# A two-layer hybrid trunk: state-space input tables built on VectorE from turned factors, the last low parts queued first, and cosine products into rotated tiles

## The chip, the cores and the metric

The kernel runs on one core of a Trainium2 chip, in one launch. The metric is the time of that launch in device microseconds (us). Engines are named as the profile names them: PE is TensorE (PEld its weight loads), DVE is VectorE, ACT is ScalarE, POOL is GpSimd, SP is SyncE, whose queue issues nearly all DMAs here. Each engine works through its own instructions in the order in which the program lists them; a scheduler in the language fixes that order when the kernel is built, from priorities and dependencies.

## The reference

Input x is (1, 1024, 1024) in float32: 1024 frames of width 1024. Each layer adds a mixer of the RMS-normalised input; a last RMS norm ends it.

```python
# layer 0: one projection feeds both branches
y_a = s5_mixer(u)            # diagonal complex state space, 64 groups of 16 inputs and 64 states,
                             #   chunks of 64 frames, then gelu and a GLU with glu_w
y_b = retention(q, k, v)     # 8 heads, q and k rotated: [x1*cos - x2*sin, x1*sin + x2*cos]
x = x + concat(y_a * silu(g_a), y_b * silu(g_b)) @ w_out
# layer 1: conformer convolution module
u = a * sigmoid(b)           # h @ w_c gives a, b and a gate
x = x + (swish(norm(causal_depthwise_conv31(u))) * silu(g)) @ w_out_c
out = rmsnorm(x)
```

The state space in closed form is: the states of a chunk are sums over its frames of powers of a complex number times an input vector (bb_re, bb_im) times u, so the kernel needs tables that are products of a power factor P and an input factor B.

## The kernel before, in words

Activations stand transposed: channels on the 128 partitions, frames along the free axis, in two halves of 512. Every projection goes block by block of 128 output channels. To reach float32 accuracy each weight block is loaded in float32 (tile wf), rounded on ACT to a high part wh, and the rest, wf − wh, is the low part wl, made by DVE or POOL; the activations are split likewise. A product is three matmuls (mm3: high by high, high by low, low by high), so a half block is 24 matmuls of 128x512 and a block 48. The list made in plan() fixes the order of the weight blocks, and wnext() starts each load two blocks ahead. wf, wh and wl have three buffers each. LO_V lists the names whose low part DVE makes; all others are POOL's. Blocks in TWICE are needed for both halves of the frames at different times: their low part is stored to DRAM the first time and loaded again (wload_again) the second. For the blocks woc3_1 and woc4_1 of the last projection this reload goes into two tiles of another pool, in two pieces each.

Layer 0 runs in stages. First come eight blocks of u, then sixteen gate blocks (g), with the state space between them: one batch of eight groups for every two gate blocks. For a batch, s5_tables makes on POOL (outer, six products and sums of 128x512 a pair) the tables Mr and Mi, Tc and Ts, W3, and s5_states uses them: TensorE turns Mr and Mi (eight transposes of 128x128 against the identity, L707), ACT copies the result to W2 (L709), and W2 times U (the batch's input, loaded from DRAM at L700) gives v. DVE rotates v by Tc and Ts, scans it along the free axis and rotates back, which gives the states S. TensorE also multiplies Mr and Mi by c (kp, L752), DVE completes it (Kg), TensorE turns it (kt, L758); it goes to DRAM and comes back as the direct table W1. s5_out of the batch before then makes y on TensorE.

Then retention: for each of four pairs of heads k and q are projected (raw), a copy with its 32-row groups swapped (swp) is made by four DMAs through SP's queue, POOL multiplies raw by the cosine and swp by the sine table, and DVE adds the two into krot or qrot, which TensorE reads in sp, ktp and ro. The core of turn() in ret_proj is

```python
for b in range(4):
    s = b ^ 1
    nc.sync.dma_start(swp[32 * b:32 * b + 32, :], raw[32 * s:32 * s + 32, :])
cs = [slice(h * HALF, (h + 1) * HALF) for h in range(2)]
for c in cs:
    nc.gpsimd.tensor_tensor(raw[:, c], raw[:, c], tab[:, 0, c], op=ALU.mult)
    nc.gpsimd.tensor_tensor(swp[:, c], swp[:, c], tab[:, 1, c], op=ALU.mult)
return o, [lambda c=c: nc.vector.tensor_tensor(o[:, c], raw[:, c], swp[:, c], op=ALU.add) for c in cs]
```

After the GLU comes the output projection (wos and wor blocks, mm_wo), then layer 1: a, b and gate blocks, the convolution with 31 taps on DVE, POOL and ACT, its norm, and the last projection mm_oc (w_out_c), whose result is added to the stored x (x1l, loaded at L1316). The last three blocks of the second half are worked in quarters of 256 frames. For each quarter final_norm sums the squares on TensorE (rf_ps), takes the root, spreads it over the partitions (a diagonal tile rf_dg and a matmul, rf_R), and multiplies the eight blocks (fo), which two by two go to the output.

Of the kernel before, what the change touches and what calls it, by code (L numbers as in the profile page):

```python
# [11 lines left out]
F32 = mybir.dt.float32  # L12
# [7 lines left out]
P = 128  # L20
D = 1024
T = 1024
KB = 8
# [6 lines left out]
WARM = 14  # L30
WAIT = 8
TWICE = ("wo", "cb", "ca", "cg")
LO_V = {f"g{i}" for i in range(1, 10)} | {"u4", "u5", "u6"}
G0 = 3
# [16 lines left out]
class Trunk:  # L51
# [22 lines left out]
    def plan(self):  # L74

        A = self.A
        seq = [(A["w_ab"][nb], f"u{nb}") for nb in range(8)]
        seq += [(A["w_ab"][nb], f"g{nb}") for nb in range(8, 24)]
        for p in range(4):
            seq += [(A["w_ab"][28 + p], f"k{p}"), (A["w_ab"][24 + p], f"q{p}")]  # L80

            if p == 0:
                seq += [(A["w_v"][j], f"v{p}_{h}_{j}") for h in range(2) for j in range(4)]
            elif p > 1:
                seq += [(A["w_v"][2 * p + i], f"v{p}_{i}") for i in range(2)]
# [15 lines left out]
        self.low_load = {}  # L101
        self.wnames, self.lo_d = {n for _, n in seq}, {}
# [10 lines left out]
    def wload(self, src, name):  # L113
# [5 lines left out]
        tiles = None  # L119
        for tiles in self.wload_pieces(src, name, 1, [self.nc.vector if name[:2] in LO_V else self.nc.gpsimd]):  # L120
            done = tiles or done
# [5 lines left out]
    def wload_again(self, src, name, low):  # L127
# [6 lines left out]
        if name in ("woc3_1", "woc4_1"):  # L134

            tiles = [self.op_tile(self.opA, "A1", f"wl{i}_{name}") for i in range(2)]
            for i, t in enumerate(tiles):
                nc.sync.dma_start(t[:].bitcast(F32), low[:, i * HALF:(i + 1) * HALF])
            return wh, Halves(tiles)
        wl = self.wp.tile([P, KB, P], F32R, name=f"wl_{name}", tag="wl", bufs=3)  # L140
        self.low_load[name[:-2]] = nc.sync.dma_start(wl[:].rearrange(fl).bitcast(F32), low)
        return wh, wl
# [83 lines left out]
    def layer0_front(self, st):  # L226
# [138 lines left out]
        for nb in range(5, 8):  # L365
            u_block(nb)
        self.s5_tab, self.s5_back, self.s5_last = {}, {}, None
        self.s5_tables(0)
        for nb in range(8, 24):
# [71 lines left out]

    def rstd(self, parts, pool, name):
# [9 lines left out]
        self.spread(rp[:, :n], r4, pool, name)  # L452
        return rp
# [201 lines left out]
    def outer(self, B, o_r, o_i, ar, ai, br, bi, view, op_r=ALU.subtract, op_i=ALU.add):  # L655

        gp = self.nc.gpsimd
        for o, op, (a0, b0), (a1, b1) in ((o_r, op_r, (ar, br), (ai, bi)), (o_i, op_i, (ar, bi), (ai, br))):
# [3 lines left out]
            yield gp.tensor_tensor(o, o, t[:], op=op)  # L662

    def s5_tables(self, B):

# [20 lines left out]
        self.s5_last = self.chained(chain(*made), self.s5_last)  # L686
        R8 = self.big(f"R8_{B}", "R8", 2)
        for q in range(4):
            nc.scalar.mul(R8[:, q, :], self.m01[:], self.r8[:, 4 * B + q:4 * B + q + 1])
        self.s5_tab[B] = Mr, Mi, W3, Tc, Ts, R8  # L690

    def s5_states(self, B):
        nc, w = self.nc, self.s5
        gp, v = nc.gpsimd, nc.vector
        q0 = 4 * B
        Mr, Mi, W3, Tc, Ts, R8 = self.s5_tab.pop(B)


        U = w.tile([P, 8, P], F32, name=f"U_{B}", tag="U", bufs=2)
        nc.sync.dma_start(U[:], self.u_d[B].rearrange("j h g m -> (j h) g m"))  # L700


        W2 = []
        for nm, M in (("r", Mr), ("i", Mi)):
            ps = self.bank(f"w2{nm}_{B}")
# [59 lines left out]
        nc.sync.dma_start(Wd[:], bass.AP(tensor=kd.tensor, offset=kd.offset, ap=[[P, P], [16 * P, 8], [1, P]]))  # L765
        W1 = w.tile([P, 8, P], F32, name=f"W1_{B}", tag="W1", bufs=2)
        nc.scalar.copy(W1[:].rearrange("p g (i h) -> p i g h", i=8), Wd[:].rearrange("p i (g h) -> p i g h", g=8))
# [74 lines left out]
    def ret_proj(self, pair):  # L842
# [15 lines left out]
        def turn(nm, behind=None):  # L858
# [3 lines left out]
            for b in range(4):  # L862
                s = b ^ 1
                nc.sync.dma_start(swp[32 * b:32 * b + 32, :], raw[32 * s:32 * s + 32, :])
            cs = [slice(h * HALF, (h + 1) * HALF) for h in range(2)]
            for c in cs:
                nc.gpsimd.tensor_tensor(raw[:, c], raw[:, c], tab[:, 0, c], op=ALU.mult)
                nc.gpsimd.tensor_tensor(swp[:, c], swp[:, c], tab[:, 1, c], op=ALU.mult)
            return o, [lambda c=c: nc.vector.tensor_tensor(o[:, c], raw[:, c], swp[:, c], op=ALU.add) for c in cs]

# [170 lines left out]
    def layer0_back_and_layer1(self, st):  # L1041
# [269 lines left out]
        def w_out_c(h, nb, cols, hold=None):  # L1311
# [10 lines left out]
            def part(c):  # L1322
                ps = self.bank(f"mm_oc{nb}_{h}_{c.start}", aux=False)
                n = c.stop - c.start
                self.gemm(ps[:, :n], w, [(a[:, c], b[:, c]) for a, b in zs[h]], hold)
                v.tensor_tensor(t[:, c], ps[:, :n], xt[:, c], op=ALU.add)
                nc.scalar.activation(sq[:, c], t[:, c], AF.Square)
# [7 lines left out]
        def final_norm(h, c):  # L1335
            n = c.stop - c.start
            end = h and c.stop == HALF
            R = lp.tile([P, HALF], F32, name=f"RF_{h}_{c.start}", tag="dg", bufs=1)
            rp = self.rstd([final[h][nb][1][:, c] for nb in ((0, KB - 1) if h else (0,))], lp, f"rf_{h}_{c.start}")
            for nb in range(8):  # L1340
                if nb == 1 and not end:
                    nc.scalar.copy(R[:, :n], rp[:, :n])
# [30 lines left out]
        for h in range(2):  # L1373
# [26 lines left out]
            with self.at(410000):  # L1400
                blocks(1, range(3))
                with self.tc.issue_after(self.last_mm.ins):
                    final_norm(0, *full)
                blocks(1, range(3, 5))
            with self.at(430000):
# [11 lines left out]
                next(last[2])  # L1417
                final_norm(1, quarters[1])

# [97 lines left out]
```

## Time and profile before

| what | value |
|---|---|
| runs | 1215.86, 1223.36, 1215.69 us (median 1215.86) |
| profiled execution | 1215.57 us, span in the profile 1213.8 us |
| mean granted clock of TensorE | 0.995 of full speed |
| busy | PE 99%, PEld 83%, DVE 62%, ACT 40%, POOL 55% |
| DMA | 227.11 MB, mean 187 GB/s |

The span runs from the first to the last instruction or transfer that the profiler saw; the execution's own time lies 1.8 us above it. A view of the waits lists what each engine stood idle for; the chain follows the work that ended last back from the end, so that a step on it is a step that delays the end; a row of the timeline gives start, duration, engine, source line, operation, what is written from what, tile sizes, and in brackets the idle time before it with what ended it. In the views of windows each engine's busy time is followed by its count of instructions, then come the granted clock, the share of DMA time and GB/s.

### The profile page before, as it was taken

The numbers are of one execution on the slowest core, as the hardware profiler recorded it, in microseconds if no ns is written. First come the engines' busy times: TensorE is split into PE (matmuls) and PEld (weight loads), VectorE is DVE, ScalarE is ACT, GpSimd is POOL, SyncE is SP. The second block draws the span as 40 slices with busy tenths as digits, with TensorE's granted clock in tenths as the row PEclk, the third lists the DMA queues.
The fourth block names the chain that finished last, engine by engine and source line by source line (L and its number), as shares of the span: only waits on it lengthen the run. The fifth ranks groups of instructions, "written<-read, shape, count | busy, mean of one in ns | idle before, by whom it ended". The sixth has DMA issues, their size and how long they took to land.

```text
span 1213.8 us, 17240 instructions
## 1 busy us (share of the span) xinstructions
PE 1196.5 (99%) x6468; PEld 1001.8 (83%) x6468; DVE 751.7 (62%) x1337; ACT 479.9 (40%) x706; POOL 663.4 (55%) x457
## 2 busy tenths in 40 slices
PE   9999999999999999999999999999999999999997
PEld 7888888888888888998888788888888888888876
DVE  7966655555412457467647101699999799999523
ACT  7212233332223222234334322545535675434652
POOL 2059988888237153243443551678453567758642
PEclk9999999999999999999999999999999999999998
DMA  8342433333385165567447877766678654366763
GB/s 334 104 139 72 148 131 127 125 128 137 107 286 174 53 208 150 164 206 256 158 140 225 284 267 255 243 208 203 216 241 278 209 190 156 113 190 228 254 246 131
DMA packets 100515, 227.11 MB, mean 187 GB/s; under 512 B 9296, under 2 KB 38224, under 8 KB 99792
## 3 DMA queue, kind: packets, MB, share of 16 engines
q1 hardware_dynamic: 100432, 226.01, 56.0%
q8 instruction: 51, 0.84, 0.3%
q14 instruction: 32, 0.26, 0.1%
HBM read 160.51 MB, written 61.28 MB: 183 GB/s over the span
## 4 chain that ended last, share of the span: by engine, by line
PE 92%; DMA 3%; DVE 2%; ACT 1%; POOL 1%; issue 1%; SPq 0%; DVEq 0%; ACTq 0%; POOLq 0%
PE mm_g L165 7%; PE mm_g L166 7%; PE mm_g L164 7%; PE mm_wo L166 5%; PE mm_wo L164 5%; PE mm_wo L165 5%; PE mm_b L165 2%; PE mm_b L166 2%; PE mm_a L165 2%; PE mm_a L166 2%; PE mm_b L164 2%; PE mm_a L164 2%; PE mm_u L166 2%; PE mm_u L165 2%; PE mm_u L164 2%; PE mm_glu L164 2%
## 5 line engine op out<-in xcount | busy, mean ns | idle before, releaser
L1214 DVE SCALAR_TENSOR_TENSOR cv<-u,convw,cv 128x512 f32<-128x512 f32 x398 | 273.3, 749 | 11.9 <-ACT cv L1200 9.6
L1194 POOL TENSOR_TENSOR tp<-tp,tp 128x512 f32<-128x512 f32 x64 | 83.0, 1297 | 44.1 <-ACT tp L1193 43.0
L166 PE MATMUL mm_g<-xh,wl_g 128*128 128x512 f32 x256 | 100.8, 394 | 0.0
L165 PE MATMUL mm_g<-xl,wh_g 128*128 128x512 f32 x256 | 100.6, 393 | 0.0
L164 PE MATMUL mm_g<-xh,wh_g 128*128 128x512 f32 x256 | 100.5, 393 | 0.0
L1193 ACT ACTIVATE tp<-u,convw 128x512 f32<-128x512 f32 x64 | 45.7, 720 | 35.4 <-POOL tp L1194 33.8
L347 DVE TENSOR_TENSOR gt<-mm_g,R 128x512 f32<-128x512 f32 x32 | 21.9, 684 | 59.9 <-PE mm_g L166 59.9
L165 PEld LDWEIGHTS mm_g<-xl,wh_g 128*128 128x128 f32 x256 | 48.1, 188 | 11.3 <-issue 1.6
L166 PE MATMUL mm_oc<-zh,wl_woc 128*128 128x512 f32 (+1 forms) x152 | 54.7, 363 | 2.7 <-DMA wl_woc<-lo_woc 2.7
L156 POOL TENSOR_TENSOR wl_v<-wf_v,wh_v 128x1024 fp32r<-128x1024 f32 x12 | 29.0, 2424 | 51.3 <-ACT wh_v L155 51.3
L166 PEld LDWEIGHTS mm_g<-xh,wl_g 128*128 128x128 f32 x256 | 48.0, 188 | 10.6
L164 PEld LDWEIGHTS mm_g<-xh,wh_g 128*128 128x128 f32 x256 | 48.1, 188 | 9.6
L164 PE MATMUL mm_oc<-zh,wh_woc 128*128 128x512 f32 (+1 forms) x152 | 55.0, 367 | 0.0
L165 PE MATMUL mm_oc<-zl,wh_woc 128*128 128x512 f32 (+1 forms) x152 | 54.4, 360 | 0.3 <-POOL zl L1039 0.3
L1114 DVE TENSOR_TENSOR x<-mm_wo,xr 128x512 f32<-128x512 f32 x16 | 11.1, 691 | 70.3 <-PE mm_wo L166 49.8
L1086 POOL TENSOR_TENSOR yg<-yg,yn 128x512 f32<-128x512 f32 x16 | 21.7, 1357 | 55.8 <-PE mm_glu L166 16.0
L166 PE MATMUL mm_wo<-yrh,wl_wor 128*128 128x512 f32 x128 | 50.0, 391 | 0.8 <-POOL wl_wor L156 0.8
L165 PE MATMUL mm_u<-xl,wh_u 128*128 128x512 f32 x128 | 50.1, 391 | 0.6 <-DVE xl L279 0.6
L164 PE MATMUL mm_g<-h1h,wh_cg 128*128 128x512 f32 x128 | 50.4, 394 | 0.0
L164 PE MATMUL mm_wo<-yrh,wh_wor 128*128 128x512 f32 x128 | 50.3, 393 | 0.0
L164 PE MATMUL mm_glu<-yh,wh_glu 128*128 128x512 f32 x128 | 50.3, 393 | 0.0
L164 PE MATMUL mm_b<-h1h,wh_cb 128*128 128x512 f32 x128 | 50.2, 392 | 0.0
(400 smaller groups left out, 3626.6 us busy)
## 6 DMA issues: line engine op xcount, KB each, us to landing
wf_g<-w_ab SPq DMA_DIRECT2D x16, 512.0 KB, 4.1
wf_wos<-w_out SPq DMA_DIRECT2D x16, 512.0 KB, 5.3
wf_wor<-w_out SPq DMA_DIRECT2D x16, 512.0 KB, 5.7
wf_cb<-w_c SPq DMA_DIRECT2D x16, 512.0 KB, 4.7
wf_ca<-w_c SPq DMA_DIRECT2D x16, 512.0 KB, 4.7
wf_woc<-w_out_c SPq DMA_DIRECT2D x16, 512.0 KB, 5.3
wf_v<-w_v SPq DMA_DIRECT2D x12, 512.0 KB, 4.7
wf_cg<-w_c SPq DMA_DIRECT2D x11, 512.0 KB, 4.5
```

What stands on the lines that cost most here:

```text
L156: lo[i].tensor_tensor(wl[:].rearrange(fl)[:, c], wf[:, c], h.bitcast(F32), op=ALU.subtract)
L164: nc.tensor.matmul(ps, wh[:, kb, :], xh, start=start, stop=False)
L165: nc.tensor.matmul(ps, wh[:, kb, :], xl, start=False, stop=False)
L166: self.last_mm = nc.tensor.matmul(ps, wl[:, kb, :], xh, start=False, stop=stop)
L347: nc.vector.tensor_tensor(gt[:, c], ps[:], self.R[:, c], op=ALU.mult)
L1086: gp.tensor_tensor(yg[:], yg[:], yn[:], op=ALU.mult)
L1114: v.tensor_tensor(t[:], ps[:], xt[:], op=ALU.add)
L1193: nc.scalar.mul(sk[:], u[:, k:k + HALF], cw[:, nb, k:k + 1])
L1194: gp.tensor_tensor(s0[:], s0[:], sk[:], op=ALU.add)
L1214: v.scalar_tensor_tensor(dst[:], *tap, accs_[i][:], op0=ALU.mult, op1=ALU.add)
```

## The change

It consists of five edits.

1. From the third batch on (B > 1) W2 is no longer turned on TensorE from Mr and Mi. s5_turned() turns the small factors once, by twelve transposes, and stores them to DRAM; s5_w2() loads them spread over the partitions (four DMAs of 256 KB a batch, listed behind the load of U) and DVE makes W2 with four products, a difference and a sum, each of 128x512. To make room, R8 and W1 have one buffer in place of two.
2. In turn() the cosine product goes into the rotated tile, ahead of the sine products; DVE adds in place.
3. The low parts of wos and wor are made by DVE.
4. The reloaded low parts of woc3_1 and woc4_1 are listed ahead of the other reloads of that kind and ahead of the x1l loads of the last three blocks.
5. The first quarter's final norm stops after four blocks and goes on behind the last sum of x; in the second quarter five matmuls of ones stand between the sums and the spreading.

```diff
+IDLE = 5
-LO_V = {f"g{i}" for i in range(1, 10)} | {"u4", "u5", "u6"}
+LO_V = {f"g{i}" for i in range(1, 10)} | {"u4", "u5", "u6", "wos", "wor"}
...
-                nc.sync.dma_start(t[:].bitcast(F32), low[:, i * HALF:(i + 1) * HALF])
+                self.early_low = nc.sync.dma_start(t[:].bitcast(F32), low[:, i * HALF:(i + 1) * HALF])
...
-        self.low_load[name[:-2]] = nc.sync.dma_start(wl[:].rearrange(fl).bitcast(F32), low)
+        with self.tc.issue_after(self.early_low.ins) if self.early_low else nullcontext():
+            self.low_load[name[:-2]] = nc.sync.dma_start(wl[:].rearrange(fl).bitcast(F32), low)
...
+        if idle:
+            wait = self.bank(f"{name}_wait", aux=False)
+            with self.tc.issue_after(self.last_stat.ins):
+                for _ in range(idle):
+                    self.last_idle = nc.tensor.matmul(wait[:, :P], self.ones[:], self.ones[:], start=True, stop=True)
...
+    def s5_turned(self):
+        self.pt_d = self.dram.tile([2, 2, P, P], F32, name="pt_d")
+        self.bt_d = self.dram.tile([2, 4, P, P], F32, name="bt_d")
+        order = [self.big(f"hq{c}", "tmpV", 4) for c in range(2)]
+        for o, t in zip(order, (self.bbr, self.bbi)):
+            nc.scalar.copy(o[:].rearrange("p a (h q) -> p (a h) q", h=4), t[:].rearrange("p q h -> p h q"))
+        for i, (dst, parts) in enumerate((...)):
+            ps = self.bank(f"turn{i}")
+            for a, src in enumerate(parts):
+                nc.tensor.transpose(ps[:, a * P:(a + 1) * P], src, self.ident[:])
+            t = self.big(f"turned{i}", "tmpV", 4)
+            nc.scalar.copy(t[:].rearrange("p q n -> p (q n)"), ps[:])
+            nc.sync.dma_start(dst, t[:])
+
+    def s5_w2(self, B):
+        (ptr, pti), (btr, bti) = ([self.big(f"{n}{c}_{B}", f"{n}{c}", 1) for c in "ri"] for n in ("PT", "BT"))
+        with self.tc.issue_after(self.u_load.ins):
+            for c, (pt, bt) in enumerate(((ptr, btr), (pti, bti))):
+                nc.sync.dma_start(pt[:].rearrange("p q n -> p (q n)"),
+                                  bass.AP(tensor=dp.tensor, offset=dp.offset + (c * 2 * P + 4 * B) * P,
+                                          ap=[[32 * P, 8], [0, 16], [1, 4 * P]]))
+                nc.sync.dma_start(bt[:].rearrange("p q n -> p (q n)"),
+                                  bass.AP(tensor=db.tensor, offset=db.offset + (c * 4 * P + 4 * B) * P,
+                                          ap=[[0, 8], [32 * P, 16], [1, 4 * P]]))
+        w2r, w2i = (self.big(f"W2{nm}_{B}", f"W2{nm}", 1) for nm in "ri")
+        v.tensor_tensor(w2r[:], ptr[:], btr[:], op=ALU.mult)
+        v.tensor_tensor(w2i[:], ptr[:], bti[:], op=ALU.mult)
+        v.tensor_tensor(ptr[:], pti[:], bti[:], op=ALU.mult)
+        v.tensor_tensor(pti[:], pti[:], btr[:], op=ALU.mult)
+        v.tensor_tensor(w2r[:], w2r[:], ptr[:], op=ALU.subtract)
+        v.tensor_tensor(w2i[:], w2i[:], pti[:], op=ALU.add)
+        return [w2r, w2i]
...
-        self.s5_tab[B] = Mr, Mi, W3, Tc, Ts, R8
+        self.s5_tab[B] = Mr, Mi, W3, Tc, Ts, R8, self.s5_w2(B) if B > 1 else None
...
-        W2 = []
-        for nm, M in (("r", Mr), ("i", Mi)):
+        first, W2 = W2 is None, W2 or []
+        for nm, M in (("r", Mr), ("i", Mi)) if first else ():
...
             for c in cs:
-                nc.gpsimd.tensor_tensor(raw[:, c], raw[:, c], tab[:, 0, c], op=ALU.mult)
+                nc.gpsimd.tensor_tensor(o[:, c], raw[:, c], tab[:, 0, c], op=ALU.mult)
+            for c in cs:
                 nc.gpsimd.tensor_tensor(swp[:, c], swp[:, c], tab[:, 1, c], op=ALU.mult)
-            return o, [lambda c=c: nc.vector.tensor_tensor(o[:, c], raw[:, c], swp[:, c], op=ALU.add) for c in cs]
+            return o, [lambda c=c: nc.vector.tensor_tensor(o[:, c], o[:, c], swp[:, c], op=ALU.add) for c in cs]
...
-            nc.sync.dma_start(xt[:], self.x1_d[rows(nb), hs(h)])
+            with self.tc.issue_after(self.early_low.ins) if h and nb > 4 else nullcontext():
+                nc.sync.dma_start(xt[:], self.x1_d[rows(nb), hs(h)])
...
             for nb in range(8):
+                if nb == 4:
+                    yield
...
                 with self.at(420000):
-                    final_norm(1, quarters[0])
+                    first = final_norm(1, quarters[0])
+                    next(first)
...
-                final_norm(1, quarters[1])
+                with self.at(425000), self.tc.issue_after(self.last_add.ins):
+                    for _ in first:
+                        pass
+                for _ in final_norm(1, quarters[1]):
+                    pass
```

More of the change, by code (lines that the diff above doesn't have):

```diff
@@ L119, in wload @@
         tiles = None
-        for tiles in self.wload_pieces(src, name, 1, [self.nc.vector if name[:2] in LO_V else self.nc.gpsimd]):
+        for tiles in self.wload_pieces(src, name, 1, [self.nc.vector if name[:2] in LO_V or name[:3] in LO_V else self.nc.gpsimd]):
             done = tiles or done
@@ L367, in layer0_front @@
         self.s5_tab, self.s5_back, self.s5_last = {}, {}, None
+        self.s5_turned()
         self.s5_tables(0)
@@ L451, in rstd @@
         rp = self.bank(f"{name}_R")
-        self.spread(rp[:, :n], r4, pool, name)
+        with self.tc.issue_after(self.last_idle.ins) if idle else nullcontext():
+            self.spread(rp[:, :n], r4, pool, name)
         return rp
@@ L1338, in final_norm @@
             R = lp.tile([P, HALF], F32, name=f"RF_{h}_{c.start}", tag="dg", bufs=1)
-            rp = self.rstd([final[h][nb][1][:, c] for nb in ((0, KB - 1) if h else (0,))], lp, f"rf_{h}_{c.start}")
+            rp = self.rstd([final[h][nb][1][:, c] for nb in ((0, KB - 1) if h else (0,))], lp, f"rf_{h}_{c.start}",
+                           IDLE if end else 0)
             for nb in range(8):
+                if nb == 4:
+                    yield
                 if nb == 1 and not end:
```

25 lines of the change are left out of this document (17 added, 8 removed).

## The prediction

> **What bounds the kernel now.** I read the page first (busy shares, chain), then TensorE's waits, then the chain that ended last in order of time, then the timelines around its few steps that are not TensorE.
>
> ```profile
> span 1213.8 us, 17240 instructions
> PE 1196.5 (99%) x6468; PEld 1001.8 (83%) x6468; DVE 751.7 (62%) x1337; ACT 479.9 (40%) x706; POOL 663.4 (55%) x457
> ...
> PE 92%; DMA 3%; DVE 2%; ACT 1%; POOL 1%; issue 1%; SPq 0%; DVEq 0%; ACTq 0%; POOLq 0%
> ```
>
> TensorE (PE) is busy 99% of the span and holds 92% of the chain. VectorE (DVE) and GpSimd (POOL) have room on average. So work that moves onto DVE costs nothing by itself, and only two things shorten the kernel: matmuls that disappear and TensorE's stalls. The stalls that this change can touch are few:
>
> ```profile
> PE mm_oc L166 <- DMA wl_woc<-lo_woc: 2.7, 2, 2.3
> PE sp L972 <- DVE qrot L869: 1.8, 1, 1.8
> PE ro L999 <- DVE sc L978: 0.9, 1, 0.9
> PE mm_wo L166 <- POOL wl_wor L156: 0.8, 1, 0.8
> PE rf_ps L421 <- DVE fo L1352: 0.6, 1, 0.6
> ```
>
> The columns are the total in us, the number of times and the longest. Together they are 6.8 us, which already caps what the change can do beside the matmuls it takes out.
>
> **Part 1: state-space tables on DVE.** A batch now turns its two input tables with eight 128x128 transposes. The rows give their price and the batch period, 303.94 − 274.43 = 29.5 us:
>
> ```profile
> 274.43 0.44 PE w2r L707 x4
> 274.87 0.44 PE w2i L707 x4
> ...
> 303.94 0.44 PE w2r L707 x4
> ```
>
> Six batches lose 0.88 us each, −5.3 us; the new s5_turned adds 12 transposes of 0.11 us, +1.3. TensorE saves **−4.0** us (−4.6 at most, if the change of shape costs 0.1 us a batch more, which no row shows alone). ScalarE loses 12 copies and gains five; it is far from the path.
>
> The price is on DVE: six 128x512 products or sums a batch, between the steps of the scan. Both their inputs lie in SBUF, and there the trace shows DVE and POOL excluding each other. In the order DVE, POOL, DVE, POOL, DVE, POOL:
>
> ```profile
> 224.53 0.69 DVE L728 TENSOR_TENSOR v<-v,Tc 128x512 f32<-128x512 f32 x1
> 226.37 1.10 POOL L660 TENSOR_TENSOR o<-s_bbi,s_pr 128x512 f32<-128x512 f32 x1
> ...
> 233.50 1.56 DVE L156 TENSOR_TENSOR wl_g<-wf_g,wh_g 128x1024 fp32r<-128x1024 f32 x1
> 233.95 2.41 POOL L660 TENSOR_TENSOR o<-s_e2i,s_e1r 128x512 f32<-128x512 f32 x1
> ...
> 441.23 2.86 DVE L869 TENSOR_TENSOR krot<-kraw,kswp 128x512 f32<-128x512 f32 x1 [1.18 <-POOL kswp L868]
> 441.16 2.38 POOL L156 TENSOR_TENSOR wl_v<-wf_v,wh_v 128x1024 fp32r<-128x1024 f32 x1
> ```
>
> The step v, with one input in PSUM, takes 0.69 us. The step krot began just after a POOL subtraction and ended 0.55 us after it: it waited, then ran. In the second pair POOL waited for DVE. So a W2 step costs 0.6 us plus what is left of the POOL operation (1.1 to 1.4 us in this stage): 0.6 to 2.0 us, and I take 1.2, with a whole wait for the one that follows another directly. DVE's sum per batch is then:
>
> ```profile
> 215.50:245.00 29.50, 29.50 (x204) 24.67 (x202) 15.66 (x23) 9.08 (x18) 23.72 (x19) 1.00 0.36 128
> ```
>
> The third and fifth busy times are DVE and POOL. DVE goes from 15.7 to about 24 us of the new period of 28.6, POOL, delayed 0.6 us by each step, from 23.7 to 27.3. Both fit. For TensorE three deadlines count after the v matmuls of a batch:
>
> ```profile
> 233.33 0.38 SPq L700 DMA_DIRECT2D U<-u_d  x1
> 1125.28 0.45 PE mm_oc L164 x2
> ```
>
> (1) kt stands after 33 gate matmuls in the changed order, 0.6 + 33 x 0.225 = 8.1 us after v; its input Kg waits behind two W2 steps on DVE and is ready at about 6.2, at 7.6 with 2.0 us a step. (2) The load of U for the next batch, now 10.1 us after v, stands on SP's queue behind the store of a gate block whose second half DVE evacuates behind all six steps: issued at about 20, landed at about 24.5 (a load took 4.6 us in part 4's rows), needed by v at 26.7. With 2.0 us a step it comes at about 27.5, up to 1 us late. (3) The four broadcast loads of 256 KB follow U and wait for the tables' last readers; they land near 26.5 and are needed at 28.7, when the first W2 step reaches the head of DVE. The weight load behind them comes some 6 us later than now, needed two blocks later. So I add nothing for stalls; the other bound is 1 us in each of six batches, +6.
>
> [...]
>
> **Part 2: the rotation.** The chain at the one stall of the attention stage:
>
> ```profile
> 444.69 5.31 DMA qswp<-qraw
> 450.31 1.13 issue
> 451.45 1.28 POOL qswp L868
> 452.73 1.25 POOL qraw L867
> 453.98 1.69 POOL qswp L868
> 455.69 2.83 DVE qrot L869
> 458.65 0.46 PE sp L972 x2
> ```
>
> After the swap lands, POOL now runs four products, since the cosine product overwrote raw in place and had to wait for the swap that reads it. Writing it into the rotated tile lets two of the four run while the swap is under way, so two of 1.25 us leave the chain: −2.5 us against a stall of 1.8: **−1.8**, margin 0.7. The new wait is that POOL's product must wait for TensorE's readers of the previous rotated pair, with weight subtractions of 2.4 us queued behind. In the changed order these products stand behind the previous pair's sine products, so I expect no stall; bounds 0 and −2.7 (with the 0.9 of ro, which hangs on another DVE queue).
>
> **Part 3: sixteen low parts to DVE.**
>
> ```profile
> L156 POOL TENSOR_TENSOR wl_wor<-wf_wor,wh_wor 128x1024 fp32r<-128x1024 f32 x8 | 19.6, 2445 | 14.5 <-PE mm_wo L166 7.2 <-ACT wh_wor L155 5.4 <-DMA lo_wor<-wl_wor 1.8
> 630.00:760.00 130.00, 128.96 (x569) 105.63 (x568) 36.39 (x47) 43.37 (x60) 53.80 (x31) 1.00 0.73 248
> ```
>
> A part takes 2.4 us on POOL; the same shape took 1.56 on DVE beside POOL (the wl_g row of part 1). DVE is busy 36 of the 130 us there and takes some 25 more. Most of the 0.8 us wait goes: **−0.7** (0 to −0.8).
>
> **Part 4: last low parts queued first.** On SP's queue the last four (L138) stood behind a load that waits for a buffer:
>
> ```profile
> 1153.38 0.33 SPq L132 DMA_DIRECT2D wf_woc<-w_out_c  x1
> 1167.26 0.32 SPq L141 DMA_DIRECT2D wl_woc<-lo_woc  x1
> 1167.63 1.85 SPq L138 DMA_DIRECT2D wl_woc<-lo_woc  x4
> ...
> 1167.63 4.62 DMA wl_woc<-lo_woc
> 1172.30 0.79 PE mm_oc L166
> 1173.09 0.43 PE mm_oc L164
> ...
> 1170.00:1175.00 5.00, 2.70 (x6) 2.15 (x7) 0.87 (x2) 3.80 (x6) 1.26 (x1) 0.67 0.92 304
> ```
>
> They are now issued right after 1153.4 and land by about 1161, before TensorE's 1170. The 2.7 us stall goes. It also goes with a clock drop: in this window the granted clock is 0.67 and a matmul takes 0.43 us where it takes 0.225 at 1125.28; from 1172.3 to 1175 that is some 1.3 us lost. The x1l loads that are moved behind are needed only from about 1177. Sum **−3.8** (−2.3 if a smaller late load remains, −4.1 at most).
>
> **Part 5: the tail.** The last sum of x now stands ahead of three of the fo products of the first quarter:
>
> ```profile
> 1202.07 1.75 DVE L1352 TENSOR_TENSOR fo<-x,rf_R 128x256 f32<-128x256 f32 x5 [0.44 <-ACT RF L1342]
> ...
> 1203.73 0.42 DVE L1326 TENSOR_TENSOR x<-mm_oc,x1l 128x256 f32<-128x256 f32 x1
> ...
> 1203.96 1.35 PE L421 MATMUL rf_ps<-ones,s2q 128*128 128x64 f32 x8 [0.65 <-DVE fo L1352]
> ...
> 1206.48 1.19 PE L440 MATMUL rf_R<-rf_dg,ones 128*128 128x256 f32 x2 [1.17 <-DVE rf_dg L438]
> ```
>
> The sum moves 0.4 us forward, but rf_ps waits for the last fo, which reads the bank it takes: three fo of 0.35 us after the sum end near 1204.85, so rf_ps starts about 1.0 later and, its eight parts then together, ends 0.8 later. Five dummy matmuls fill the 1.28 us before rf_R. If they keep the clock, rf_R takes 0.6 instead of 1.19 us; if the clock drops under them they delay it. Bounds −0.6 and +1.8; I take **+0.9**.
>
> **Sum.** −4.0 − 1.8 − 0.7 − 3.8 + 0.9 = −9.4 us. The profiled execution took 1215.57 us, 1.8 outside its span, and is 0.3 below the median 1215.86 of the runs. That gives 1206.2 on its scale and 1206.5 on the median's, 0.8% faster. A measurement of this kernel can tell about 1% from no change (below 1203.7, above 1228.0).
>
> **Rivals.** (a) *More than that.* Every part is at its better bound: −4.6 − 2.7 − 0.8 − 4.1 − 0.6 = −12.8, 1203.1 on the median's scale, just past the mark of 1%. For it: no row forbids any of them. Against: it needs all at once, and the waits quoted above leave nothing further to gain. Chance 0.12.
> (b) *Part of the gain turns into new waits.* The U loads are within 2.2 us of their deadline; with the +6 of part 1 the time is 1212.5, with half of it and half of the two stalls of parts 2 and 4 back 1212, so 1209 to 1214. For it: the krot row. Against: POOL idles 5.8 of 29.5 us per batch, so not every step meets it. Chance 0.22.
> (c) *Slower: DVE becomes the bound of the state-space stage.* With d us a step, DVE needs 15.7 + 6d of 28.6 us, so it decides from d = 2.15; at 2.4 the six batches lose 9 us and the gain is gone. At the 2.86 of krot, if every step meets an operation as long, they lose 25 us: 1231.8 with the other gains kept. For it: krot and qrot do wait so. Against: POOL's operations in this stage are 1.1 to 1.4 us, not 2.4. Chance 0.11.
> (d) *The early queue does nothing*: the low parts wait for their own tiles or for bandwidth; then part 4 brings nothing and the time is 1210.3. For it: 1.0 MB lands in one stretch at 304 GB/s in the quoted window. Against: at 1153 nothing but one weight load stands before them. Chance 0.05, inside the range.
>
> **How the numbers follow.** The forecast, 1203.7 to 1209, has 0.50. The range 1203 to 1219 holds it with (b), (d) and nearly all of (a) and the beginning of (c), leaving out some 0.12. The chances of faster by over 1%, within 1% and slower by over 1% are 0.10 (most of a), 0.81 and 0.09 (most of c).
>
> **What would show it.** Right: no w2r rows from the third batch on; no sp<-qrot, mm_oc<-DMA and mm_wo<-wl_wor rows in TensorE's waits; a granted clock of 1.00 around 1160 to 1170; W2 steps of about 1.2 us and a period of 28.6. Wrong: TensorE waiting at v for U, at kt for Kg or at v for W2; W2 steps over 2 us; a new DMA wait behind the moved x1l; the tail from the last gate of mm_oc to the end longer by over 2 us.

## The result, and the profile after

Six runs of the changed kernel took 1203.16 to 1205.3 us, median 1204.53; those of the kernel before beside them have a median of 1216.09. The ratio is 0.9892, 95% interval [0.9871, 0.9914]: 1.1% faster, 13.1 us by the ratio and 11.6 by the medians. A second set in a later comparison gave 0.9898 [0.9879, 0.9918]. The forecast time of 1206.5 us is 2.0 too long and the direction is right. My main case is wrong: the change can be told from none, since neither interval comes near 1.00, and both ratios lie just past the 1% that I said it would stay within. How far past is not settled: both intervals reach over the 1% mark, and by the medians alone the change is 0.95%.

The page after, busy shares and chain:

```profile
span 1203.5 us, 17285 instructions
PE 1191.8 (99%) x6442; PEld 999.4 (83%) x6442; DVE 799.5 (66%) x1389; ACT 477.5 (40%) x699; POOL 637.9 (53%) x441
...
PE 95%; DMA 2%; DVE 1%; ACT 1%; issue 0%; POOL 0%; SPq 0%; DVEq 0%; POOLq 0%; ACTq 0%
```

The profiled execution took 1205.3 us, 10.3 less than the one profiled before. TensorE's share of the chain that ended last went from 92 to 95%, and DVE is busier by 48 us without costing anything. TensorE's waits, all of them:

```profile
PE rf_ps L424 <- DVE fo L1412: 1.6, 1, 1.6
PE idle L257 <- DVE mhalf L203: 1.1, 1, 1.1
PE mm_oc L168 <- DMA wl_woc<-lo_woc: 1.0, 2, 0.7
PE mm_u L167 <- DVE xl L281: 1.0, 1, 1.0
PE mm_oc L167 <- POOL zl L1095: 0.5, 1, 0.5
PE ro L1055 <- DVE sc L1034: 0.5, 1, 0.5
```

The rows of sp, wl_wor and the 2.3 us of lo_woc are gone; rf_ps grew from 0.6 to 1.6, as foreseen. In the state-space stage, one new period of 28.65 us (columns as before: the third and fifth busy times are DVE and POOL), and DVE's steps in it:

```profile
215.50:244.15 28.65, 28.65 (x195) 23.85 (x197) 22.79 (x28) 8.12 (x16) 25.40 (x19) 1.00 0.58 177
...
217.52 0.68 DVE L710 TENSOR_TENSOR W2r<-PTr,BTr 128x512 f32<-128x512 f32 x1
220.62 1.59 DVE L711 TENSOR_TENSOR W2i<-PTr,BTi 128x512 f32<-128x512 f32 x1
222.13 1.07 DVE L810 TENSOR_TENSOR Kg<-Kg,s_s_dd 128x16 f32<-128x16 f32 x1
224.32 0.76 DVE L712 TENSOR_TENSOR PTr<-PTi,BTi 128x512 f32<-128x512 f32 x1
227.25 1.05 DVE L713 TENSOR_TENSOR PTi<-PTi,BTr 128x512 f32<-128x512 f32 x1
228.23 1.77 DVE L714 TENSOR_TENSOR W2r<-W2r,PTr 128x512 f32<-128x512 f32 x1
232.90 1.62 DVE L715 TENSOR_TENSOR W2i<-W2i,PTi 128x512 f32<-128x512 f32 x1
```

The six steps take 0.7 to 1.8 us, 1.25 on average (forecast 1.2): those that meet a POOL operation wait for its end (W2i at 220.62 ends 0.55 us after a POOL operation that ended at 221.66), and the difference right behind a product waits longest, 1.75 to 1.91 us in all six batches. DVE needs 22.8 us of the period, POOL 25.4 (forecast 24 and 27.3). The tail after:

```profile
1193.46 1.07 DVE L1412 TENSOR_TENSOR fo<-x,rf_R 128x256 f32<-128x256 f32 x3
...
1194.68 1.08 PE L424 MATMUL rf_ps<-ones,s2q 128*128 128x64 f32 x8 [1.60 <-DVE fo L1412]
1195.59 1.33 PE L457 MATMUL rf_wait<-ones 128*128 128x128 f32 x10
...
1196.93 0.67 PE L443 MATMUL rf_R<-rf_dg,ones 128*128 128x256 f32 x2
```

### The profile page after: what moved, and what is told of

Its sections match the earlier page's. It is cut to its first block, busy times and chain, and to the rows that moved or that the text cites. A ratio compares the mean times of both kernels' runs of the same rounds, so it can differ in the third digit from the quotient of the medians.

```text
span 1203.5 us, 17285 instructions
## 1 busy us (share of the span) xinstructions
PE 1191.8 (99%) x6442; PEld 999.4 (83%) x6442; DVE 799.5 (66%) x1389; ACT 477.5 (40%) x699; POOL 637.9 (53%) x441
## 4 chain that ended last, share of the span: by engine, by line
PE 95%; DMA 2%; DVE 1%; ACT 1%; issue 0%; POOL 0%; SPq 0%; DVEq 0%; POOLq 0%; ACTq 0%
PE mm_g L166 7%; PE mm_g L167 7%; PE mm_g L168 7%; PE mm_wo L168 5%; PE mm_wo L166 5%; PE mm_wo L167 5%; PE mm_b L167 2%; PE mm_b L168 2%; PE mm_a L167 2%; PE mm_a L168 2%; PE mm_b L166 2%; PE mm_a L166 2%; PE mm_u L168 2%; PE mm_u L167 2%; PE mm_u L166 2%; PE mm_glu L166 2%
## 5 line engine op out<-in xcount | busy, mean ns | idle before, releaser
L1270 DVE SCALAR_TENSOR_TENSOR cv<-u,convw,cv 128x512 f32<-128x512 f32 x398 | 273.4, 751 | 11.9 <-ACT cv L1256 9.6
L393 POOL TENSOR_TENSOR s1q<-s1q,s1q 128x512 f32<-128x512 f32 x12 | 17.5, 1455 | 78.2 <-ACT s1q L388 78.2
L168 PE MATMUL mm_a<-h1h,wl_ca 128*128 128x512 f32 x128 | 50.2, 392 | 0.0
```

The costliest lines, as they stand in the source:

```text
L168: self.last_mm = nc.tensor.matmul(ps, wl[:, kb, :], xh, start=False, stop=stop)
L393: nc.gpsimd.tensor_tensor(a, a, sq[:], op=ALU.add)
L1270: v.scalar_tensor_tensor(dst[:], *tap, accs_[i][:], op0=ALU.mult, op1=ALU.add)
```

## A table of stages

A time to 0.2% does not say which part brought what. So I compare, for each profiled execution, the start of the same matmuls. Each column is a stretch between two of them (ss is the first sum of squares; the other names are those of the text above), each number how much longer (+) or shorter (−) that stretch is than in the first profile of the kernel before, in us.

| execution | start to ss | state space, to y of the last batch | to mm_q behind sp | to mm_glu behind ro | output projection, to r_ps | to mm_oc | mm_oc, first waits | mm_oc, lo_woc stall, to rf_ps of the third quarter | to the last rf_ps | end |
|---|---|---|---|---|---|---|---|---|---|---|
| before, second | −0.4 | 0.0 | −1.6 | −0.4 | −0.5 | −0.1 | +0.9 | −1.4 | 0.0 | 0.0 |
| before, third | +0.8 | 0.0 | +2.2 | −0.2 | +0.4 | −0.1 | +0.8 | +0.2 | 0.0 | −0.6 |
| edit 1 alone | +0.1 | −3.9 | −0.2 | −0.9 | −0.1 | +0.8 | +0.4 | −2.0 | 0.0 | −0.8 |
| edit 2 alone | +0.2 | 0.0 | −2.0 | −0.5 | −0.7 | 0.0 | +1.0 | +0.2 | 0.0 | 0.0 |
| edit 3 alone | +0.4 | 0.0 | −0.2 | −0.2 | −1.9 | −0.1 | +0.8 | −1.2 | 0.0 | 0.0 |
| edit 3, second | +0.8 | 0.0 | +1.0 | −0.4 | −1.9 | −0.1 | +0.3 | +0.1 | 0.0 | −0.5 |
| edit 4 alone | +1.0 | 0.0 | −0.3 | +0.2 | +0.3 | −0.1 | +1.5 | −4.0 | 0.0 | 0.0 |
| changed | +0.5 | −3.9 | −2.0 | −0.4 | −1.9 | +0.1 | +1.3 | −4.0 | +1.0 | −1.0 |
| changed, second | −0.2 | −3.9 | −2.0 | −1.0 | −1.9 | +0.1 | +2.6 | −4.0 | +1.0 | −1.1 |
| without edit 1 | +0.3 | 0.0 | −1.8 | +0.3 | −1.3 | +0.1 | +1.2 | −4.0 | +1.0 | +0.1 |
| without the matmuls of ones | +0.4 | −3.9 | −2.0 | −0.4 | −1.9 | +0.2 | +1.1 | −4.0 | +1.0 | −0.4 |
| without edit 4 | +0.8 | −3.9 | −2.0 | −0.4 | −1.9 | +0.4 | +0.3 | −0.6 | +1.0 | −0.3 |
| own bank | +0.1 | −3.9 | −2.0 | −0.7 | −1.9 | +0.3 | +1.3 | −4.0 | −0.8 | −0.3 |
| own bank, made low | +0.2 | −3.9 | −2.0 | −0.5 | −1.9 | +0.1 | +0.2 | −4.0 | −0.8 | −0.2 |

Two things are to be seen. The state-space stage, which has no stall, repeats to 0.1 us. What varies between executions of one kernel is mostly the cost of its stalls: 3.8 us at sp, 1.6 at lo_woc and 0.9 in the output projection among three executions of the kernel before. The start varies by 1.2 and the end by 0.6 us.

## The experiments

**The edits one by one.** Each is the kernel before with the hunks of one edit of the change.

Edit 1:

> The kernel before with edit 1 alone (W2 on DVE from the third batch on). Theory A, the parts add up and each is worth what its own stage shows: the state-space stage ends 3.9 us earlier (six periods of 28.65 instead of 29.5, less 1.3 for the twelve new transposes) and the whole time falls by the same 3.9, to about 0.997 of before; the stalls at sp, wl_wor and lo_woc stay at 1.8, 0.8 and 2.3 us. Theory B, a later wait takes the gain: one of these stalls is anchored to work that does not move with TensorE and grows by up to 3.9, the ratio is 1.000. A W2 step takes 1.2 us on average under both.

Measured 1210.51 us, 0.9945 [0.9927, 0.9964]. The stage shows the 3.9 us of theory A, the whole is 6.7 less by the ratio and 5.7 by the medians. In the profile 0.9 of the rest lies at ro and 2.0 at lo_woc, where the stall was 1.6 us and the clock was kept; but the kernel before without any edit had −1.4 there in its second execution, so most of the 2.0 can be scatter. A repeat in more rounds:

> The kernel before with edit 1 alone, timed again in more rounds. In four runs it was 0.9945 of before, 6.7 us, where its stage shows 3.9. Theory A: 3.9 us is all that it brings by itself, and the rest was the scatter of the waits that stay; now about 0.9968. Theory C: ending the stage 3.9 us earlier also shortens the later waits (ro lost its 0.9, the lo_woc wait fell from 2.3 to 1.6 with no clock drop); then 0.9945 again, and the same two differences in the second trace.

0.9949 [0.9934, 0.9964], 6.2 us by the ratio: again more than 3.9 us, which would be 0.9968 and lies just outside both intervals. Theory A as I put it falls, by a narrow margin. There is no second trace to look for theory C's two differences: the profiled execution took 4251 us, with matmuls every 0.84 us in place of 0.227 at a granted clock of 1.000, for a reason that the record does not show. It is left out of the ratio and of the table; the nine others took 1208.8 to 1213.9 us.

Edit 2:

> The kernel before with edit 2 alone (cosine products into the rotated tile). Theory A: the 1.8 us wait of sp for qrot is gone, mm_q after it starts 2.0 us earlier against the state-space stage's end, the time falls by 2.0 to 2.4 us (0.998). Theory B: the ro wait of 0.9 for sc or the loads behind POOL's new wait take it over, under 1 us is left.

1213.7 us, 0.9977 [0.9960, 0.9993], 2.5 us by the medians, and −2.0 at sp: theory A.

Edit 3:

> The kernel before with edit 3 alone (low parts of wos and wor on DVE). My prediction gave it 0.7 us, the 0.8 us row of wl_wor. Theory A, from the gaps between matmuls in both traces: three gaps at 672 to 675 us of 0.2, 0.4 and 0.95 us and the slow restarts behind them, 1.9 us in all, go with it, since ACT's rounding of wos waited for the same POOL queue: 1.9 us (0.9985). Rival: only the wl_wor gap goes, 0.8, and the other 1.1 us of the two traces' difference came with parts 1 and 2, which move the weight loads.

The rows of the kernel before that it removes (timeline of TensorE, the idle time and what ended it in brackets):

```profile
673.06 0.50 PE L164 MATMUL mm_wo<-ysh,wh_wos 128*128 128x512 f32 x1 [0.21 <-ACT wh_wos L155]
674.58 0.50 PE L166 MATMUL mm_wo<-yrh,wl_wor 128*128 128x512 f32 x1 [0.78 <-POOL wl_wor L156]
```

Neither is in the new trace, and the stage is 1.9 us shorter. But ten runs gave 1216.41 us, 0.9998 [0.9983, 1.0012], whose lower end only just reaches 1.9 us. A second profiled execution:

> The kernel before with edit 3 alone, a second profiled execution. Its first trace showed 1.9 us gone at mm_wo, but its runs were no faster than before (0.9998) and had a mean granted clock of 0.994 where the profiled one had 0.997. Theory: the 1.9 us are gone here too and the loss is in half-clock windows behind the sp and lo_woc stalls that stay. Rival: the loss lies in the output projection itself, where DVE makes the low parts.

1214.9 us; the 1.9 us are gone here too, so the rival (a loss inside the output projection) falls. The sp wait was 2.0 us and its stretch 1.0 longer, and a clock drop stands at lo_woc. That such losses ate the gain in the ten runs fits their mean clock of 0.994 (before 0.996), but was not shown run by run. So edit 3 by itself is worth 1.9 us in the traces and shows no gain in the runs, and that stays open.

Edit 4:

> The kernel before with edit 4 alone (last low parts queued first). Theory A: the 2.3 us wait of mm_oc and the half clock of about 3.4 us after it go (granted clock 1.00 all through 1165 to 1180), 3.0 to 4.0 us less between the last cst and rf_R; the three smaller waits ahead (wl_woc twice, zl) stay at 0.3 to 0.7 and are not this edit's. Rival: the edit itself brings the new waits of 0.7 and 0.4 us for wl_woc and the longer one for zl that the changed kernel's trace shows at 1145 to 1152, since its loads share the queue; then they are here too and about 2.7 us is left.

1214.26 us, 0.9975 [0.9958, 0.9992]; −4.0 at lo_woc, and +1.5 at the first waits. The last is no cost of the edit: in the table all executions but two have 0.3 to 1.5 there (2.6 in one of the changed kernel, 0.2 where two of these low parts are not loaded at all), with the edit or without it; the first profile had the least. The rival falls.

Edit 5:

> The kernel before with edit 5 alone (order of the tail, five matmuls of ones). Theory A, from the two traces: rf_ps starts 1.0 us later because it waits for the last fo, its passes then run together, and rf_R at full clock takes 0.68 instead of 1.2 us: the stretch from the last sum of x to the end changes by +0.3, the time by no more than the runs scatter (0.999 to 1.001). Rival, my forecast's term: +0.9 us. Third: the kept clock is worth more than the rows show, the time falls by over 1 us.

1217.65 us, 1.0006 [0.9989, 1.0022]: no gain by itself. The interval holds theory A's +0.3 us and my +0.9 (1.0007) alike and does not decide between them. In its profile rf_R took 1.11 us, not theory A's 0.68, and the stretch from the last matmul of mm_oc to the end was 11.4 us where the first profile has 10.8. The profile is an odd one: the granted clock is shown as 0.95 in stretches without any stall, though the matmuls of mm_b follow each other every 0.227 us as in the first profile. It is left out of the table.

**The kernel before, twice more.**

> The kernel before once more, for a second profiled execution. The stage table of the first eight profiles says that the one my sum was made from waited little: 0.3 us at the first wl_woc wait where four others with the same code waited 1.2 to 1.9, and no clock drop at the sp wait. Theory: a second execution is 1 to 4 us longer, and the difference lies at those two waits and in the half-clock windows behind the stalls of sp, wl_wor and lo_woc, not in the busy stages. Rival: the stages themselves vary, for instance the state-space stage by over 0.5 us.

> The same again, a third execution of the kernel before: the waits at sp, wl_wor and lo_woc come every time with 1 to 2.5 us, the half clock behind each in some executions only.

1212.12 and 1219.1 us, 7 us apart with the same code. Part of what I expected failed: the second execution was 3.5 us shorter than the first, not longer, and had no sp wait at all. The third against the first in the windows around the sp stall (granted clock is the third number from the end); the first three rows are the third execution, its waits below them:

```profile
455.00:460.00 5.00, 2.99 (x45) 2.48 (x44) 3.84 (x3) 0.00 (x0) 4.36 (x3) 1.00 0.39 92
460.00:465.00 5.00, 4.94 (x23) 3.81 (x25) 3.90 (x10) 0.00 (x0) 0.00 (x0) 0.66 1.02 279
465.00:470.00 5.00, 5.00 (x58) 4.64 (x57) 4.07 (x21) 0.60 (x2) 4.32 (x4) 1.00 0.15 54
...
PE mm_oc L166 <- DMA wl_woc<-lo_woc: 2.6, 2, 2.3
PE sp L972 <- DVE qrot L869: 2.1, 1, 2.1
```

A stall of 2.1 us at sp put the clock to half for (1 − 0.66) x 5 / 0.5 = 3.4 us, and by the starts of the same matmuls TensorE lost 1.5 us more behind it. In the first profile the same stall of 1.8 us cost no clock (1.00 in that window), and in the second there was no stall at all. A 2.2 to 2.4 us stall at lo_woc halved the clock in some executions (before, before third, edit 2) and not in others (before second, edit 3).

The clock records of the traces show more of what decides. The drops begin a whole number of steps of 3.413 us after the trace's first clock record: 133 steps in the third execution (6.44 to 460.41 us), 342 and 352 in the first (4.38 to 1171.74 and to 1205.87), 350 in the changed kernel (6.95 to 1201.62). So I cut the traces into these steps, here around the sp stall of the third execution and the 2.4 us stall at lo_woc of edit 3 (the first busy time is TensorE):

```profile
457.00:460.41 3.41, 1.34 (x18) 1.09 (x18) 3.27 (x3) 0.00 (x0) 2.36 (x2) 1.00 0.70 183
460.41:463.82 3.41, 3.41 (x9) 2.70 (x9) 2.85 (x8) 0.00 (x0) 0.00 (x0) 0.50 1.03 279
...
1166.36:1169.77 3.41, 2.44 (x15) 1.83 (x13) 1.04 (x2) 3.41 (x5) 0.00 (x0) 1.00 0.73 227
1169.77:1173.18 3.41, 1.97 (x8) 1.61 (x9) 0.87 (x2) 2.88 (x5) 1.26 (x1) 1.00 0.89 302
```

In the third execution the whole stall falls into one step, 2.07 us idle, and the next step runs at half clock. With edit 3 a longer stall is divided, 0.97 and 1.44 us idle, and the clock stays. Over sixteen traces (all but those of edit 5 alone and of the 4251 us), a step at full clock with about 1.9 us idle or more was always followed by half clock, one with 1.26 or less never, and between them both occur: 1.60 us was followed by half clock in three steps and by full clock in three. In the first execution the step of the lo_woc stall (1168.33 to 1171.74) had 1.78 us idle and the one around rf_ps (1202.46 to 1205.87) 1.27, and half clock followed both; it did not follow the 1.46 us around sp there (454.94 to 458.35), nor the 1.60 us around rf_ps of the changed kernel (1191.38 to 1194.79). So it matters in these traces how a step's border cuts a stall; what decides between 1.3 and 1.9 us stays open. The scatter lies where the theory put it, mostly in the stalls and the clock behind them.

**The changed kernel without one edit.**

> The changed kernel without edit 1 (edits 2 to 5 alone). Theory A: 3.9 us longer than the changed kernel in the stage and in all, about 0.9925 of before, and few half-clock windows, as the long stalls are gone. Theory C: 6 us longer, 0.994, as the ro and wl_woc waits come back larger.

1209.48 us, 0.9940 [0.9921, 0.9959], against 1203.97 of the changed kernel in the same comparison: edit 1 is worth 5.5 us there by the medians. Of the 6.2 us between the profiles 3.9 lies in its stage, 0.7 at ro, 0.6 in the output projection, 0.2 at sp and 1.1 at the end, where the clock fell (see the tail below). So the size is theory C's, but of its two waits only ro came back, not wl_woc. Over all traces in the table the ro wait is 0.3 to 1.3 us without edit 1 and 0 to 0.5 with it, and the lo_woc stall of the traces without edit 4 is 2.2 to 2.4 us without edit 1 and 1.5 to 1.6 with it. Why an earlier end of the state space shortens them stays open. The ro wait hangs on ACT and DVE behind the load of wf_glu, where I changed nothing; in this trace one DVE step there (sg) took 1.45 us where the changed kernel's took 0.71.

> The changed kernel without edit 4. The lo_woc stall of 2.3 to 2.5 us comes back; with it, in some executions, half a window of clock, 1.2 to 1.4 us more. Theory A: 2.5 to 4 us longer than the changed kernel, 0.992 of before, and the runs scatter more than the 2 us of the changed kernel. Rival: the stall is shorter because the other edits moved the queue, under 1.5 us.

1206.86 us, 0.9919 [0.9898, 0.9940], 2.9 more than the changed kernel: theory A, though the stall is 1.5 us and not 2.3 to 2.5. The stall and the window behind it:

```profile
1164.78 0.56 PE L167 MATMUL mm_oc<-zh,wl_woc 128*128 128x512 f32 x1 [1.53 <-DMA wl_woc<-lo_woc]
...
1165.00:1170.00 5.00, 5.00 (x16) 3.92 (x16) 0.87 (x2) 2.10 (x4) 0.67 (x1) 0.66 1.00 365
```

Sixteen matmuls in 5 us, where at 0.225 us a piece 22 fit. Of its six runs three have a mean clock of 0.995 and take 1207.4 to 1209.7 us, three have 0.999 and take 1205.6 to 1206.3: without edit 4 the kernel loses about 2 or about 4.5 us, as the clock stays or goes. In the profile, one of the slower three, 3.4 of this lie at lo_woc and 0.7 at the end, where the clock fell too.

> The changed kernel again, as the common measure of this call: 0.989 of before, no stall over 1.6 us, granted clock 0.999, a spread of 2 us.

1203.97 us, 0.9898, a spread of 1.5 us; one stall was over the 1.6 us: 1.8 at wl_woc, and the clock was at half behind it from 1149.6 to 1153.0. So the changed kernel still has a stall that can cost its clock.

**Where the slower rival begins.**

```diff
-        v.tensor_tensor(w2r[:], ptr[:], btr[:], op=ALU.mult)
-        v.tensor_tensor(w2i[:], ptr[:], bti[:], op=ALU.mult)
-        v.tensor_tensor(ptr[:], pti[:], bti[:], op=ALU.mult)
+        for _ in range(3):
+            v.tensor_tensor(w2r[:], ptr[:], btr[:], op=ALU.mult)
+        for _ in range(3):
+            v.tensor_tensor(w2i[:], ptr[:], bti[:], op=ALU.mult)
+        for _ in range(3):
+            v.tensor_tensor(ptr[:], pti[:], bti[:], op=ALU.mult)
```

> The changed kernel with the first three W2 products of a batch made three times each (the same values written again): twelve W2 steps a batch in place of six. Tests the slower rival of the forecast. DVE is busy 22.3 us of the period of 28.65 us; at 1.2 to 1.3 us a step it needs 29.5 to 30.1. Theory: DVE becomes the bound of the stage, the period grows to about 30, six batches lose 5 to 9 us, and the whole is 0.994 to 0.998 of before. Rival: SP's queue and kt bound it earlier, as the store of the gate block and U wait behind the steps: 2 to 4 us a batch, 12 to 25 us, 1.00 to 1.01 of before. If nothing changes (0.989), the price of 1.2 us a step does not add.

1232.69 us, 1.0126 [1.0100, 1.0153]: 28 us over the changed kernel, 4.7 a batch. TensorE's two longest waits and a window of 35 us:

```profile
PE kt L815 <- DVE Kg L813: 12.3, 4, 4.0
PE v L775 <- issue: 7.9, 3, 6.1
...
220.00:255.00 35.00, 32.33 (x230) 26.77 (x227) 33.90 (x35) 8.79 (x16) 29.24 (x19) 1.00 0.40 139
```

DVE is busy 33.9 of 35 us, and kt waits for Kg behind the steps. The chain that ended last holds no TensorE instruction between 235.9 and 264.5 us: it runs through DVE, with a load of PTr just ahead. In the changed kernel it is all TensorE from 158 to 301 us. So DVE has become the bound, as the theory says, but with five periods of 31.5 to 35.5 us, 33 on average, in place of 30: the steps take 1.33 us, not 1.25, and the load of PTr, whose only buffer the steps of the batch before still read, is on the chain too. The 28 us are more than the 5 to 9 of the theory and the 12 to 25 of its rival. The changed kernel stands before this point: six steps have room, twelve do not.

**The tail.**

```diff
-IDLE = 5
+IDLE = 0
```

> The changed kernel without the five matmuls of ones. If they hold the clock, TensorE's clock falls to half before rf_R, which takes 1.2 us instead of 0.68, and the end comes 0.5 us later. Rival: the clock of the tail depends on where its window falls and not on these matmuls; then rf_R is the same and the end 0.1 us earlier.

1205.3 us, 0.9896 [0.9867, 0.9925]. The row of rf_R against the 0.67 above, and the window of the tail:

```profile
1196.86 1.19 PE L443 MATMUL rf_R<-rf_dg,ones 128*128 128x256 f32 x2 [1.17 <-DVE rf_dg L441]
...
1195.00:1204.00 9.00, 1.88 (x8) 1.00 (x7) 3.33 (x10) 0.26 (x1) 0.00 (x0) 0.52 0.48 164
```

The clock is 0.52 where it was 0.89, rf_R takes 1.19 us, and from the last matmul of mm_oc to the end it is 11.3 us in place of 10.7. That looks as if the five matmuls hold the clock, but the steps of 3.41 us and the other traces say otherwise. The steps of this trace, and the tail of the kernel without edit 1, which has the five matmuls:

```profile
1192.00:1195.41 3.41, 1.81 (x16) 1.64 (x15) 1.86 (x6) 0.92 (x2) 1.18 (x2) 1.00 0.66 223
1195.41:1198.82 3.41, 1.47 (x4) 0.59 (x3) 1.32 (x5) 0.26 (x1) 0.00 (x0) 0.50 0.24 84
...
1200.67 2.11 PE L456 MATMUL rf_wait<-ones 128*128 128x128 f32 x10
1202.58 1.06 PE L442 MATMUL rf_R<-rf_dg,ones 128*128 128x256 f32 x2
```

Without the five matmuls the clock fell at 1195.41, behind the 1.6 us wait of rf_ps; the first of them would have started 0.9 us after rf_ps, at 1195.45, too late to prevent it. With them it fell all the same in three traces (edit 5 alone, without edit 1, without edit 4), where they took 1.6 to 2.1 us and rf_R 1.06 to 1.11. And without them rf_R took 0.67 in three traces of the old order (before third, edit 1 alone, edit 3 second). So this run does not show that they hold the clock. The rival's clock that doesn't depend on them fits all these traces; its forecast of an unchanged rf_R failed, as this execution lost its clock earlier than the changed kernel's.

Like for like, edit 5 costs time. Where rf_R ran at full clock, the stretch from the last matmul of mm_oc to the end is 10.0 to 10.2 us in the old order and 10.7 in the changed kernel; where it ran at half clock, 10.7 to 10.8 and 11.4 to 11.9.

```diff
-        ps = self.bank(f"{name}_ps")
+        ps = self.bank(f"{name}_ps", aux=not idle)
```

> The changed kernel with the last sums (rf_ps of the last quarter) in a bank of the matmul pool, so that they don't wait for the fo that read the shared bank. In the changed kernel rf_ps waits 1.6 us for fo; its other input, the square of the last sum, is ready about 0.7 us earlier. Theory: the 1.6 us row goes, rf_ps starts 0.6 us earlier, the tail is 0.6 us shorter. Rival: the next wait (ACT's square) comes last at the same time and the gain is under 0.2 us. The profile also gives another sample of the waits of mm_oc for wl_woc, 1.0 us in the changed kernel's first trace.

1203.51 us, 0.9884 [0.9860, 0.9908], 1.0 under the changed kernel of the first comparison, which the intervals can't tell from nothing:

```profile
1192.30 0.55 PE L424 MATMUL rf_ps<-ones,s2q 128*128 128x64 f32 x4
...
1193.43 0.66 PE L424 MATMUL rf_ps<-ones,s2q 128*128 128x64 f32 x4 [0.57 <-ACT s2q L1384]
```

The first half now runs under the last sum and only the second waits, for ACT's square; the tail is 1.1 us shorter in the table, with rf_R at full clock in both: more than either theory.

```diff
+MADE = ("woc1_1", "woc2_1")
-        if twice and name.endswith("_1"):
+        if twice and name.endswith("_1") and name not in MADE:
...
-        if twice and name.endswith("_0"):
+        if twice and name.endswith("_0") and key + "_1" not in MADE:
```

(and DVE makes the names in MADE)

> The changed kernel with the last sums in their own bank and the low parts of woc1_1 and woc2_1 made by DVE from wf and wh in place of being stored and loaded again. The remaining wait of 1.0 to 1.2 us of mm_oc for wl_woc should go, since DVE makes a part 1.2 us after the buffer comes free where the load takes about 7: 1202.3 us, 0.987 of before. Rival: the two extra DVE operations sit in the chain that makes zl, and the zl wait of 0.3 to 0.5 us grows by as much: 1203.5, no gain over the own bank.

1202.83 us, 0.9886 [0.9866, 0.9905], the lowest median of all, and the first waits fall from +1.3 to +0.2 us in the table:

```profile
PE mm_oc L169 <- DVE wl_woc L159: 1.0, 1, 1.0
```

A wait of 1.0 us remains, now for DVE. Against the own bank the medians are 0.7 us shorter and the ratios equal (0.9886 and 0.9884), in different comparisons: whether it gains is not shown.

## Why the prediction was right or wrong

**Part 1** was right by its steps: −3.9 in the stage for −4.0, steps of 1.25 us for 1.2, Kg ready 5.8 us after v (223.2 − 217.4) for 6.2, kt 8.2 after v for 8.1 (the forecast's own terms give 8.0), U issued 18.8 after v for 20, no stall at v or kt. Wrong was that the stage is all: the comparisons of the whole give 5.1 to 6.7 us, by medians or ratios. The traces put some of the rest in shorter waits at ro and lo_woc; why these get shorter is open.

**Part 2**: −2.0 for −1.8, the stall gone as reasoned. Unpriced was that the stall also takes the clock in some executions (1.5 us more in the third).

**Part 3** failed as a term: 1.9 us in the traces for 0.7, beyond the 0.8 that I gave as its bound. I counted the wl_wor row alone. The second row above and the slow restarts behind both (0.33 to 0.34 us from the start of the first matmul to the next, where it is 0.23 ahead of them) belong to the same late POOL queue. In the runs of edit 3 alone this gain does not show.

**Part 4**: −4.0 at its place, near the upper end of my bound of 4.1, and 2.9 between whole kernels; 3.8 lies between. The 2.7 us that I wrote down for the stall contained a first wait of 0.4 us that this edit doesn't touch.

**Part 5**: the profiled pair shows 0 for +0.9, and this is luck. rf_ps came 1.0 later as I said; but the first profile had half clock at rf_R (1.19 us) and the changed kernel's had full clock (0.67), which gave 1.0 back. At the same clock the new tail is 0.5 to 1.2 us longer, as I had put it. The five matmuls are not shown to have any part in it.

**The sum.** The terms of the profiled pair are −3.9 − 2.0 − 0.4 − 1.9 − 2.7 + 0.0 for parts 1 and 2, ro, part 3, the first waits with part 4, and the tail; with +0.6 for the start and the rest this makes −10.3 against my −9.4. Part 3 was 1.2 us more than I said and the tail, by its clock, 0.9 better, while the first waits went 1.3 us the other way. So the forecast time came out near partly because these offset each other.

**The step that failed** is the pricing of TensorE's stalls by the rows of one view of the waits. I summed the rows to 6.8 us and called that a cap; rival (a) then says that the quoted waits leave nothing further to gain, and on this rests the 0.81 on "within 1%". My own part 4 already went over the row, 3.8 us for 2.7, by the half clock behind it; parts 2 and 3 got the row alone. In place of the 0.7 us of part 3 the traces show 1.9, and a 2.1 us stall at sp costs 1.5 us more when the clock falls. Removing the stalls and the transposes brought 11.6 us by the medians and 13.1 by the ratio, where the pair of traces shows 10.3. The waits of one execution are one draw: the kernel before lies at 1215.8 to 1218.6 us in different comparisons and scatters over 7 us among three profiles, 6.3 of it in three stalls and the clock behind them. A forecast 2.8 us from the 1% line, with terms that uncertain, should have put near half on either side. How much of the runs' gain belongs to each part beyond its own stage stays open, for parts 1 and 3 above all.

**The rivals**: (c) is real but far (w2_twice, twelve steps a batch); (b) and (d) did not come, apart from the 1.0 us more at rf_ps.

## What to carry to other kernels

Where TensorE bounds a kernel, price a stall from several executions: its own length varies, and the clock drop behind it comes in some of them and cost 1.5 us where the stall was 2.1. Compare a stretch at the same clock before saying what an edit there is worth. Sum the gaps between matmuls around a stall, with the slow restarts, rather than the one row that a view of the waits names. Work can be moved to a half idle engine if its steps fit ahead of the small operations that others wait for: count the deadline of each (Kg before kt), and with it the engine's whole sum and the loads that wait for its last reader.

## What the runs showed of the hardware that I had not expected

A stall of 1.5 us was enough to halve the clock for 3.4 us in one execution (without edit 4), while 2.4 us did not in another (edit 3 alone). They differ in how the stall lies to the steps of 3.413 us on which the clock drops placed above begin: 1.53 us idle within one step, against 0.97 and 1.44 in two. For steps with 1.3 to 1.9 us idle the traces show both outcomes, and what decides there is open. Five small matmuls of ones put ahead of rf_R did not keep the clock in three traces of eight: rf_R took 1.06 to 1.11 us there and 0.67 in the changed kernel's first trace.
